# One 512-column matmul for hi and lo of an operand, in a float32 decoder trunk

## The chip, the core and the metric

The kernel runs on one core of one Trainium2 chip. Its time is the device time of one execution in microseconds (us). Engines are named as the profile names them: PE is the tensor engine's matmul, PEld its weight load, DVE the vector engine, ACT the scalar engine, POOL is GpSimd, and SP issues the DMAs.

## The reference

A trunk of two layers over 256 tokens of 2048 features, all in float32. The first mixer is a Conformer convolution, the second an attention with shared K and V (16 query heads, 4 K/V heads of 128 features); after each comes a squared-ReLU MLP with a hidden layer of 8192.

```python
def reference(x, ...):                      # cut to what matters
    h = x
    h = h + conformer_conv(rmsnorm(h, norm_mix[0]), ...)        # y @ w_in, gate, 31 taps, layernorm, silu, @ w_out
    h = h + sq_relu_mlp(rmsnorm(h, norm_mlp[0]), ...)           # relu(y @ w1) ** 2 @ w2
    k_sh, v_sh = shared_kv(h, kv_norm, w_kv, cos, sin)
    h = h + dilated_attn_layer(rmsnorm(h, norm_mix[1]), k_sh, v_sh, attn_w_q[0], attn_w_o[0], cos, sin)
    h = h + sq_relu_mlp(rmsnorm(h, norm_mlp[1]), ...)
    return rmsnorm(h, final_norm)
```

## The kernel before

Activations lie feature-major: tile k of an activation holds features 128k to 128k+127 on the partitions and the 256 tokens along the free dimension. Weights come as chunks of 1 MB: [128, 16 x 128] float32 holds all 2048 inputs of 128 output features. The list `order` fixes their sequence: 32 chunks of w_in, 16 of w_out, 128 of the first MLP, 4 for K, 4 for V, 16 of w_q, 16 of w_o and 128 of the second MLP.

A product is made exact to about float32 by splitting both operands, v = hi + lo, where hi is v rounded to the one-pass format float32r. `split_upto` does that for a chunk: ACT writes hi (L138), DVE or, for the chunks in POOL_LO, GpSimd writes lo (L140). `split_into` and `scaled_split` do the same for an activation tile, which then is [128, 2, 256]: hi in the first 256 columns, lo in the second (L205, L206, L211, L212). `product` adds, for each of the 16 K tiles, three matmuls of 256 columns into one half of a PSUM bank: hi weights times hi, hi weights times lo (L193, L194), lo weights times hi (L195).

A PSUM tile `ps` is one bank, [128, 512] float32; there are eight. Weight buffers are eleven: four chunks are split ahead (LOOK), up to three are raw (RAWS). So hi of the chunk four ahead is written when the product now ending has given its own buffers back.

In `mlp`, the hidden layer is made in four quarters. A quarter is 16 products of the up half (`in_m_in`), each followed by `finish` (DVE L516: relu times the norm's scale; ACT L518: square; split into a tile of `hid`), then 16 products of the down half (`in_m_out`), each added to the residual stream `h` by `add_residual` (DVE L477). The down half's first product needs all 16 `hid` tiles. `project` runs the output product of a mixer: its first four output tiles advance together over 13 K tiles, as the operand is made, and the other tiles follow one by one. In the attention each pair of heads takes two products; a product is copied out by ACT (L673), rotated by four DVE operations (`rotate`, L558 to L561), and later scored (PE L620).

The program is recorded in source order, and a scheduler then sets the order on each engine; where rows below show an engine's order, it is the scheduler's.

Of the kernel before, what the change touches and what calls it, by code (L numbers as in the profile page):

```python
# [18 lines left out]
P = 128  # L19
D = 2048  # L20
T = 256
KT = D // P          # feature tiles of the residual stream
# [7 lines left out]
FQ = 4               # quarters of the MLP's hidden layer  # L30
# [4 lines left out]
# Columns of the packed per-feature vectors: 16 feature tiles each.  # L35
# [5 lines left out]
LOOK = 4             # weight chunks split ahead of the one in use  # L41
RAWS = 3             # weight chunks on their way or waiting to be split
N0 = 4               # output tiles of a product that starts while its operand is still being made
LAST = 13            # K tiles before this one run for all of those

# The first mixer. Its products and its depthwise convolution keep every engine busy, so:
S1_PLAIN = {0, 1, 2, 3, 4, 5, 11, 28}   # chunks of its first product that run as float32
POOL_LO = (set(range(36)) - {28}) | set(range(183, 202, 2))   # chunks (here and in the attention) that GpSimd splits
SLOTS = 8            # partial sums of the convolution that one reduction adds up
# Per reduction: taps that ScalarE multiplies, and how many of them GpSimd adds to others, which makes  # L50
# room for as many more.
PIECES = [(6, 1), (5, 2)]
PE_TAPS = {15: (18, [(6, 1)])}   # feature tiles with taps on the tensor engine: how many, and their PIECES
DIAGS = {11: [15]}   # during which tile those taps' diagonals are made
Y_SPLIT = {0: 2, 1: 9, 2: 16}   # operand tiles that are split by the end of a feature tile
SHIFT = 10           # feature tiles whose mean is the LayerNorm's provisional one
CENTER = {12: [0, 3, 7], 13: [1, 2, 5, 6], 14: [4, 12, 13], 15: [8, 9, 10, 11, 14, 15]}   # when tiles are centered
AHEAD = {13: 31, 14: 34, 15: 34}   # chunks split after a feature tile's gate, where not the next tiles'
# [3 lines left out]
def decoder_kernel(ctx, tc, xT, vec, rope, mask, w_in, w_out, w_k, w_v, w_q, w_o, m_in, m_out, out):  # L62
    """Activations lie feature-major: tile k of a [2048, 256] activation holds features
    128k..128k+127 on the partitions and the 256 tokens along the free dimension. A weight chunk
    [128, 16, 128] holds all of K for 128 output features, so one PSUM tile [128, 256] accumulates
    over its 16 K tiles.

    float32 products: both operands are split exactly, v = hi + lo, hi = v rounded to float32r's 12
    significant bits and lo = v - hi (which has 12 at most), and x.w = xh.wh + xl.wh + xh.wl, each an
    exact one-pass product that is summed in float32. What is left, xl.wl, is below float32's last  # L70
    place of x.w. Attention's own products and a part of the first one, where the vector engine is
    short of time, run as plain float32.
    """
# [30 lines left out]
    def load():  # L104
        """Load as many chunks as there is room for. Those that are not split take a split one's place."""
# [15 lines left out]
    def free(split):  # L121
        live[split] -= 1
        load()

    def split_upto(n):
        """Make the chunks before the n-th ready for use."""
        while len(ready) < min(len(order), n):
            load()
            i = len(ready)
# [42 lines left out]
    def col(name, f):  # L172
        c = VCOL[name] + f
        return vecs[:, c:c + 1]
# [593 lines left out]
```

## Time and profile before

| | |
|---|---|
| time, median of 3 runs (range) | 2118.87 us (2116.08 to 2118.92) |
| span of the profiled execution | 2114.3 us; the runs' times lie 1.8 to 4.6 us above it |
| PE busy | 2058.0 us, 97% of the span |
| DVE / ACT / POOL busy | 59% / 45% / 10% |
| granted PE clock, mean | 0.991 of 2.4 GHz |
| DMA | 368 MB, mean 174 GB/s |

Busy time of PE counts a matmul from its start to its modelled end, so two that follow each other overlap in the records; what a matmul costs is the distance from its start to the next one's start.

### The profile page before, as it was taken

What the parts mean: (1) busy time and instruction counts of PE and PEld (TensorE: products, weight loads), DVE (VectorE), ACT (ScalarE), POOL (GpSimd) and SP (SyncE); (2) the same over time, 40 slices, a digit from 0 to 9 for tenths busy, and PEclk for the clock granted to TensorE, in tenths of its full rate; (3) what the DMA queues carried; (4) which work ended last, traced back from release to release, by engine and by line L of the source; (5) the groups of instructions that cost most, each with busy time, mean ns of one, the idle gap of its engine ahead of it and who ended that gap; (6) DMA issues with size and microseconds to landing.
All of it is one profiled execution on the core that took longest, in us unless ns stands there. A gap on an engine that the chain in (4) does not pass through costs nothing.

```text
span 2114.3 us, 37655 instructions
## 1 busy us (share of the span) xinstructions
PE 2058.0 (97%) x16630; PEld 2032.8 (96%) x16630; DVE 1256.0 (59%) x1499; ACT 955.6 (45%) x1192; POOL 213.0 (10%) x83
## 2 busy tenths in 40 slices
PE   8989799999999999999999999999999999999997
PEld 7888799999999999999999889999999999999997
DVE  7999975554554455445565876555455445545553
ACT  4677664443343344344453554444344334434442
POOL 2687500000000000000003220000000000000000
PEclk9999899999999999999999999999999999999999
DMA  7344235555555555555444334555455545555552
GB/s 285 140 146 153 102 127 186 181 188 182 180 182 188 188 180 180 184 189 186 180 180 179 140 140 149 190 180 180 180 183 189 187 179 181 184 190 184 180 181 79
DMA packets 51619, 368.01 MB, mean 174 GB/s; under 512 B 5856, under 2 KB 5856, under 8 KB 7552
## 3 DMA queue, kind: packets, MB, share of 16 engines
q1 hardware_dynamic: 51312, 365.60, 48.1%
q8 instruction: 130, 2.13, 0.4%
q14 instruction: 33, 0.27, 0.0%
q10 hardware_dynamic: 144, 0.01, 0.0%
HBM read 363.49 MB, written 2.10 MB: 173 GB/s over the span
## 4 chain that ended last, share of the span: by engine, by line
PE 49%; issue 36%; DVE 12%; ACT 2%; POOL 0%; POOLq 0%; DVEq 0%; ACTq 0%
PE ps L193 16%; PE ps L194 15%; PE ps L195 15%; DVE ps L329 3%; DVE prod L335 2%; DVE act L335 2%; DVE sh L559 1%; ACT hi L138 1%; ACT prod L303 1%; DVE prod L329 1%; DVE act L361 0%; PE ps L620 0%; PE ps L593 0%; PE ps L591 0%; PE ps L592 0%
## 5 line engine op out<-in xcount | busy, mean ns | idle before, releaser
L193 PE MATMUL ps<-act,hi 128*128 128x256 f32 x5312 | 1507.5, 284 | 2.7 <-ACT act L205 2.7
L195 PE MATMUL ps<-act,lo 128*128 128x256 f32 x5312 | 1502.2, 283 | 3.0 <-DVE lo L140 3.0
L194 PE MATMUL ps<-act,hi 128*128 128x256 f32 x5312 | 1501.6, 283 | 0.0
L138 ACT CAST hi<-raw 128x2048 fp32r<-128x2048 f32 x336 | 640.0, 1905 | 948.8 <-PE ps L194 791.6
L194 PEld LDWEIGHTS ps<-act,hi 128*128 128x128 f32 x5312 | 1018.0, 192 | 0.6
L195 PEld LDWEIGHTS ps<-act,lo 128*128 128x128 f32 x5312 | 1014.2, 191 | 3.7 <-DVE lo L140 3.4
L193 PEld LDWEIGHTS ps<-act,hi 128*128 128x128 f32 x5312 | 1013.3, 191 | 3.9 <-ACT act L205 3.1
L140 DVE TENSOR_TENSOR lo<-raw,hi 128x2048 fp32r<-128x2048 f32 x298 | 682.9, 2292 | 395.9 <-ACT hi L138 395.8
L477 DVE TENSOR_TENSOR h<-ps,h 128x256 f32<-128x256 f32 x144 | 61.0, 424 | 214.0 <-PE ps L195 213.8
L140 POOL TENSOR_TENSOR lo<-raw,hi 128x2048 fp32r<-128x2048 f32 x38 | 175.0, 4609 | 126.5 <-ACT hi L138 66.3
L226 POOL TENSOR_TENSOR rc<-ms,neg_half 128x2 f32<-128x2 f32 x5 | 3.6, 729 | 1703.4 <-DVE ms L255 1703.4
L516 DVE SCALAR_TENSOR_TENSOR t<-ps,t 128x256 f32<-128x256 f32 x128 | 54.2, 425 | 161.5 <-PE ps L195 161.5
L303 ACT ACTIVATE prod<-u,vecs 128x256 f32<-128x256 f32 x217 | 90.5, 497 | 58.0 <-DVE u L397 53.8
L329 DVE SCALAR_TENSOR_TENSOR ps<-u,vecs,ps 128x256 f32<-128x256 f32 x197 | 79.6, 483 | 0.0
L199 PE MATMUL ps<-act,raw 128*128 128x256 f32 x256 | 59.4, 393 | 6.5 <-DVE act L280 6.5
L199 PEld LDWEIGHTS ps<-act,raw 128*128 128x128 f32 x256 | 50.3, 198 | 13.7 <-DVE act L280 6.5
L206 DVE TENSOR_TENSOR act<-t,act 128x256 fp32r<-128x256 f32 x144 | 60.3, 420 | 0.9 <-ACT act L205 0.9
L205 ACT CAST act<-t 128x256 fp32r<-128x256 f32 x144 | 58.6, 407 | 4.5
L335 DVE TENSOR_REDUCE prod<-prod 128x256 f32<-128x2048 f32 x15 | 58.1, 3873 | 1.6 <-ACT prod L303 0.5
L518 ACT ACTIVATE t<-t 128x256 f32<-128x256 f32 x128 | 52.7, 412 | 4.8 <-DVE t L516 4.8
L335 DVE TENSOR_REDUCE act<-prod 128x256 f32<-128x1536 f32 (+1 forms) x16 | 47.0, 2939 | 0.4
L243 ACT ACTIVATE t<-h 128x256 f32<-128x256 f32 x80 | 31.5, 407 | 28.2 <-DVE h L477 22.2
(103 smaller groups left out, 600.9 us busy)
## 6 DMA issues: line engine op xcount, KB each, us to landing
raw<-in_m_in SPq DMA_DIRECT2D x128, 1024.0 KB, 4.8
raw<-in_m_out SPq DMA_DIRECT2D x128, 1024.0 KB, 4.8
raw<-in_w_in SPq DMA_DIRECT2D x31, 1024.0 KB, 4.9
raw<-in_w_out SPq DMA_DIRECT2D x16, 1024.0 KB, 4.9
raw<-in_w_q SPq DMA_DIRECT2D x16, 1024.0 KB, 4.8
raw<-in_w_o SPq DMA_DIRECT2D x16, 1024.0 KB, 4.8
raw<-in_w_k SPq DMA_DIRECT2D x4, 1024.0 KB, 5.1
raw<-in_w_v SPq DMA_DIRECT2D x4, 1024.0 KB, 4.9
```

The source lines that it names most:

```text
L138: nc.scalar.copy(out=hi, in_=raw)
L140: eng.tensor_tensor(out=lo, in0=raw, in1=hi.bitcast(F32), op=ALU.subtract)
L193: nc.tensor.matmul(ps, lhsT=wh, rhs=a[:, 0, :], start=k == 0, stop=False)
L194: nc.tensor.matmul(ps, lhsT=wh, rhs=a[:, 1, :], start=False, stop=False)
L195: nc.tensor.matmul(ps, lhsT=wl, rhs=a[:, 0, :], start=False, stop=k == KT - 1)
L199: nc.tensor.matmul(ps, lhsT=w[:, k * P:(k + 1) * P], rhs=act_of(k), start=k == 0, stop=k == KT - 1)
L205: nc.scalar.copy(out=a[:, 0, :], in_=src)
L206: nc.vector.tensor_tensor(out=a[:, 1, :], in0=src, in1=a[:, 0, :].bitcast(F32), op=ALU.subtract)
L303: nc.scalar.activation(out=buf[:, i, :], in_=u[:, j:j + T], func=AF.Copy, scale=tap(c, j))
L329: nc.vector.scalar_tensor_tensor(out=a if j < TAPS - 2 else last[:, i % 2, :], in0=x, scalar=tap(c, j), in1=a, op0=ALU.mult, op1=ALU.add)
L335: nc.vector.tensor_reduce(out=dst, in_=buf[:, :n, :].rearrange("p j t -> p t j"), axis=AX.X, op=ALU.add)
L477: nc.vector.tensor_tensor(out=h[:, f, :], in0=ps, in1=h[:, f, :], op=ALU.add)
```

## The change

`product` now passes the whole activation tile, hi and lo side by side, under the hi weights in one matmul of 512 columns, and then hi under the lo weights in one of 256 columns, which adds to the first half of the bank. The second half of the bank holds hi weights times lo. Whoever reads a product adds the halves: `joined` (ACT copies the second half, DVE adds the first) in the MLP's `finish`, for K and for the query heads; the residual additions become two DVE additions each. The old `product` stays as `product3` for the 24 split chunks of w_in; the V product, which never used it, is as it was.

```diff
     def product(ps, w, acts, ks):
+        hi, lo = w
+        for k in ks:
+            wh, wl = hi[:, k * P:(k + 1) * P], lo[:, k * P:(k + 1) * P]
+            a = acts[k]
+            nc.tensor.matmul(ps, lhsT=wh, rhs=a.rearrange("p i t -> p (i t)"), start=k == 0, stop=False)
+            nc.tensor.matmul(ps[:, :T], lhsT=wl, rhs=a[:, 0, :], start=False, stop=k == KT - 1)
+
+    def joined(dst, ps):
+        nc.scalar.copy(out=dst, in_=ps[:, T:])
+        nc.vector.tensor_tensor(out=dst, in0=ps[:, :T], in1=dst, op=ALU.add)
+
+    def product3(ps, w, acts, ks):
         hi, lo = w
...
-                product(ps[:, :T], (hi, lo), y_hl, range(KT))
+                product3(ps[:, :T], (hi, lo), y_hl, range(KT))
...
     def add_bias_residual(f, ps):
-        nc.vector.scalar_tensor_tensor(out=h[:, f, :], in0=ps, scalar=col("bout", f), in1=h[:, f, :],
+        nc.vector.scalar_tensor_tensor(out=h[:, f, :], in0=ps[:, T:], scalar=col("bout", f), in1=h[:, f, :],
                                        op0=ALU.add, op1=ALU.add)
+        nc.vector.tensor_tensor(out=h[:, f, :], in0=ps[:, :T], in1=h[:, f, :], op=ALU.add)
 
     def add_residual(f, ps):
-        nc.vector.tensor_tensor(out=h[:, f, :], in0=ps, in1=h[:, f, :], op=ALU.add)
+        for half in (ps[:, T:], ps[:, :T]):
+            nc.vector.tensor_tensor(out=h[:, f, :], in0=half, in1=h[:, f, :], op=ALU.add)
...
                 r = tmp()
-                nc.vector.scalar_tensor_tensor(out=r, in0=ps, scalar=0.0, in1=rb, op0=ALU.max, op1=ALU.mult)
+                joined(r, ps)
+                nc.vector.scalar_tensor_tensor(out=r, in0=r, scalar=0.0, in1=rb, op0=ALU.max, op1=ALU.mult)
...
-                nc.vector.tensor_tensor(out=ks[:, i, :], in0=ps[:, :T], in1=rb, op=ALU.mult)
+                joined(ks[:, i, :], ps)
+                nc.vector.tensor_tensor(out=ks[:, i, :], in0=ks[:, i, :], in1=rb, op=ALU.mult)
                 rotate(ks[:, i, :])
...
         q = q_of[p][:, i % 2, :]
-        nc.scalar.copy(out=q, in_=ps[:, :T])
+        joined(q, ps)
         rotate(q)
```

In the changed kernel `joined` is L199 (ACT) and L200 (DVE), the wide matmul L194, the narrow one L195; the split's L205 and L206 become L220 and L221, the MLP's L516 and L518 become L534 and L536, and L477 becomes L494.

The scheduler also orders things anew. The first place is PE where a quarter of the MLP passes from its up half to its down half; `ps_8466` (before) and `ps_7074` (of the change) are the down half's first product, `ps_8522` and `ps_7115` its second, `act_8457` and `act_7065` the last `hid` tile, `act_7017` the last but one. Before:

```order
L195 MATMUL ps_8522<-act_7775,lo_8337 128x256
L193 MATMUL ps_8522<-act_7837,hi_8336 128x256
L194 MATMUL ps_8466<-act_8457,hi_8274 128x256
L195 MATMUL ps_8466<-act_8457,lo_8275 128x256
L194 MATMUL ps_8522<-act_7837,hi_8336 128x256
L195 MATMUL ps_8522<-act_7837,lo_8337 128x256
```

Of the change:

```order
L194 MATMUL ps_7115<-act_7017,hi_6972 128x512
L195 MATMUL ps_7115<-act_7017,lo_6973 128x256
L194 MATMUL ps_7074<-act_7065,hi_6924 128x512
L195 MATMUL ps_7074<-act_7065,lo_6925 128x256
L194 MATMUL ps_7115<-act_7065,hi_6972 128x512
L195 MATMUL ps_7115<-act_7065,lo_6973 128x256
```

Before, PE turns to the first product's last K tile after a third of the second product; in the change it does so only after 15 K tiles of the first and 15 of the second, and K tile 14 of the first stands behind 10.5 of the second. All eight quarters look like this.

The second place is ACT at the end of the same up half, where `hi_8460` and `hi_7068` are the hi of the chunk four ahead and `t_8453` and `t_7059` the last product's relu. Before:

```order
L138 CAST hi_8398<-raw_8216 128x2048
L518 ACTIVATE t_8393<-t_8391 128x256
L205 CAST act_8395<-t_8393 128x256
L138 CAST hi_8460<-raw_8278 128x2048
L518 ACTIVATE t_8455<-t_8453 128x256
L205 CAST act_8457<-t_8455 128x256
```

Of the change:

```order
L138 CAST hi_7068<-raw_6928 128x2048
L536 ACTIVATE t_7015<-t_7011 128x256
L199 COPY t_7059<-ps_7026 128x256
L220 CAST act_7017<-t_7015 128x256
L536 ACTIVATE t_7063<-t_7059 128x256
L220 CAST act_7065<-t_7063 128x256
```

Before, the square and the split of a `hid` tile follow right behind the hi of one chunk; in the change the copy of the last product stands behind that hi and the square of the tile before it.

The third place is DVE over the same stretch. Before:

```order
L516 SCALAR_TENSOR_TENSOR t_8453<-ps_8404,t_3800 128x256
L140 TENSOR_TENSOR lo_8461<-raw_8278,hi_8460 128x2048
L206 TENSOR_TENSOR act_8457<-t_8455,act_8457 128x256
L477 TENSOR_TENSOR h_75<-ps_8466,h_75 128x256
L140 TENSOR_TENSOR lo_8517<-raw_8340,hi_8516 128x2048
L477 TENSOR_TENSOR h_75<-ps_8522,h_75 128x256
L140 TENSOR_TENSOR lo_8573<-raw_8402,hi_8572 128x2048
```

Of the change:

```order
L140 TENSOR_TENSOR lo_7069<-raw_6928,hi_7068 128x2048
L200 TENSOR_TENSOR t_7059<-ps_7026,t_7059 128x256
L221 TENSOR_TENSOR act_7017<-t_7015,act_7017 128x256
L534 SCALAR_TENSOR_TENSOR t_7059<-t_7059,t_3528 128x256
L221 TENSOR_TENSOR act_7065<-t_7063,act_7065 128x256
L494 TENSOR_TENSOR h_75<-ps_7074,h_75 128x256
L494 TENSOR_TENSOR h_75<-ps_7115,h_75 128x256
L494 TENSOR_TENSOR h_75<-ps_7074,h_75 128x256
L494 TENSOR_TENSOR h_75<-ps_7115,h_75 128x256
L140 TENSOR_TENSOR lo_7110<-raw_6976,hi_7109 128x2048
L140 TENSOR_TENSOR lo_7151<-raw_7024,hi_7150 128x2048
```

Before, the relu was read from PSUM ahead of the chunk's lo; in the change the reading stands behind that lo, and the next two chunks' lo stand behind the residual additions of the down half's first two products.

## Rows read from the trace of the kernel before

**Rows 1.** The page: busy time by engine, and the chain that ended last.

```profile
PE 2058.0 (97%) x16630; PEld 2032.8 (96%) x16630; DVE 1256.0 (59%) x1499; ACT 955.6 (45%) x1192; POOL 213.0 (10%) x83
...
PE 49%; issue 36%; DVE 12%; ACT 2%; POOL 0%; POOLq 0%; DVEq 0%; ACTq 0%
```

**Rows 2.** Stages: us, busy and count of PE, PEld, DVE, ACT, POOL; clock; DMA.

```profile
235.00:290.00 55.00, 44.61 (x285) 42.24 (x284) 46.01 (x84) 31.89 (x65) 13.05 (x7) 0.81 0.13 45
...
368.00:1100.00 732.00, 732.00 (x6126) 732.00 (x6125) 378.50 (x352) 301.81 (x290) 0.69 (x1) 1.00 0.52 184
...
1330.00:2090.00 760.00, 760.00 (x6360) 760.00 (x6359) 387.46 (x356) 312.14 (x300) 0.69 (x1) 1.00 0.51 179
```

**Rows 3.** Groups of instructions, whole span: count, busy us, mean ns, idle before.

```profile
L193 PE MATMUL ps<-act,hi 128*128 128x256 f32 x5312 | 1507.5, 284 | 2.7 <-ACT act L205 2.7
...
L138 ACT CAST hi<-raw 128x2048 fp32r<-128x2048 f32 x336 | 640.0, 1905 | 948.8 <-PE ps L194 791.6 <-issue 115.1 <-PE ps L195 22.4
...
L477 DVE TENSOR_TENSOR h<-ps,h 128x256 f32<-128x256 f32 x144 | 61.0, 424 | 214.0 <-PE ps L195 213.8
...
L212 DVE SCALAR_TENSOR_TENSOR act<-h,vecs,act 128x256 fp32r<-128x256 f32 x64 | 29.5, 478 | 0.0
...
L673 ACT COPY act<-ps 128x256 f32<-128x256 f32 x16 | 5.9, 368 | 25.7 <-PE ps L195 25.7
```

**Rows 4.** Timeline of PE in the V product: start, duration (us), 512-column matmuls.

```profile
1122.71 0.40 PE L591 MATMUL ps<-hi,act 128*128 128x512 f32 x1
...
1123.41 0.40 PE L591 MATMUL ps<-hi,act 128*128 128x512 f32 x1
...
1143.96 0.39 PE L591 MATMUL ps<-hi,act 128*128 128x512 f32 x1
...
1144.64 0.28 PE L193 MATMUL ps<-act,hi 128*128 128x256 f32 x1
```

**Rows 5.** Timeline of PE in w_in's first, plain float32 chunks.

```profile
29.68 1.67 PE L199 MATMUL ps<-act,raw 128*128 128x256 f32 x7
```

**Rows 6.** Timeline around the end of a product in an MLP's up half.

```profile
1000.97 0.28 PE L195 MATMUL ps<-act,lo 128*128 128x256 f32 x1
1000.97 0.19 PEld L193 LDWEIGHTS ps<-act,hi 128*128 128x128 f32 x1
...
1001.09 0.28 PE L193 MATMUL ps<-act,hi 128*128 128x256 f32 x1
...
1001.17 1.91 ACT L138 CAST hi<-raw 128x2048 fp32r<-128x2048 f32 x1 [3.08 <-PE ps L194]
...
1001.29 0.42 DVE L516 SCALAR_TENSOR_TENSOR t<-ps,t 128x256 f32<-128x256 f32 x1 [1.29 <-PE ps L195]
...
1002.98 0.41 ACT L518 ACTIVATE t<-t 128x256 f32<-128x256 f32 x1
...
1003.10 2.29 DVE L140 TENSOR_TENSOR lo<-raw,hi 128x2048 fp32r<-128x2048 f32 x1 [1.39 <-ACT hi L138]
...
1003.42 0.41 ACT L205 CAST act<-t 128x256 fp32r<-128x256 f32 x1
...
1005.31 0.42 DVE L206 TENSOR_TENSOR act<-t,act 128x256 fp32r<-128x256 f32 x1
```

**Rows 7.** Timeline of one pair of heads in the attention, PE, POOL and DVE.

```profile
1204.77 4.60 POOL L140 TENSOR_TENSOR lo<-raw,hi 128x2048 fp32r<-128x2048 f32 x1 [11.27 <-PE ps L644]
...
1205.47 4.18 DVE L559 TENSOR_TENSOR sh<-sh,ropes 32x256 f32<-32x256 f32 x1
...
1209.03 0.59 PE L620 MATMUL ps<-ks,act 128*128 128x256 f32 x2
...
1210.02 0.41 DVE L561 TENSOR_TENSOR act<-act,sh 32x256 f32<-32x256 f32 x1
...
1210.58 1.11 PE L620 MATMUL ps<-ks,act 128*128 128x256 f32 x6 [0.95 <-DVE act L561]
```

**Rows 8.** DMA issues: MLP chunks, KB each, us from issue to landing.

```profile
raw<-in_m_in SPq DMA_DIRECT2D x128, 1024.0 KB, 4.8
```

More of the change, by code (lines that the diff above doesn't have):

```diff
@@ L492, in project @@
         ws = [take() for _ in range(N0)]
-        pss = [ps_tile()[:, :T] for _ in range(N0)]
+        pss = [ps_tile() for _ in range(N0)]
         for k in steps:
@@ L503, in project @@
         for f in range(N0, KT):
-            finish(f, take(), ps_tile()[:, :T], range(KT))
+            finish(f, take(), ps_tile(), range(KT))
             refill()
@@ L524, in mlp @@
                 ps = ps_tile()
-                product(ps[:, :T], take(), acts, range(KT))
-                waiting.append(ps[:, :T])
+                product(ps, take(), acts, range(KT))
+                waiting.append(ps)
                 if q == 0 and f == 0:
@@ L536, in mlp @@
                 ps = ps_tile()
-                product(ps[:, :T], take(), hid, range(KT))
-                add_residual(f, ps[:, :T])
+                product(ps, take(), hid, range(KT))
+                add_residual(f, ps)
                 if q == FQ - 1:
@@ L569, in decoder_kernel @@
         ps = ps_tile()
-        product(ps[:, :T], take(), kv_acts, range(KT))
+        product(ps, take(), kv_acts, range(KT))
         waiting.append((g, ps))
@@ L670, in decoder_kernel @@
         ps = ps_tile()
-        product(ps[:, :T], take(), acts, range(KT))
+        product(ps, take(), acts, range(KT))
         q = q_of[p][:, i % 2, :]
-        nc.scalar.copy(out=q, in_=ps[:, :T])
+        joined(q, ps)
         rotate(q)
```

## The prediction

> **What bounds the kernel now.** I read the page's busy times first. PE has 97% of the span, DVE 59%, ACT 45%, and the chain that ended last is mostly PE and "issue", with DVE at 12% [rows 1]. An average can hide stages, so the table by stage came next. In the long MLP stretches PE has no idle time at all: 6126 matmuls in 732 us, 6360 in 760 us, one every 119.5 ns at the full clock of 2.4 GHz (granted 1.00); DVE is busy about half of that time, DMA too [rows 2]. So in the MLPs, 256 of the 368 chunks, the time is the number of matmul starts times their distance, and nothing else. The end of w_in and the start of w_out (235 to 290 us) is another matter: PE is busy 44.6 of 55 us at a mean clock of 0.81, with DVE at 46 us; there PE waits for its operand [rows 2].
>
> The distance is therefore the price that matters, not the 284 ns that a record lasts [rows 3]. 256 columns at 2.4 GHz are 106.7 ns, so 12.8 of the 119.5 ns are a surplus that each matmul pays. Whether it belongs to the matmul or to its columns decides this change. The V product answers that: its matmuls are of the new kind, 512 columns of float32r, each under freshly loaded weights. 96 of them run from 1122.71 to 1144.64 us, 228.4 ns each; the fastest stretch gives (1144.64 - 1143.96) / 3 = 227 ns, the slowest (1123.41 - 1122.71) / 3 = 233 ns [rows 4]. 512 columns are 213.3 ns, so the surplus is 15 ns, about that of a 256-column matmul: it belongs to the matmul.
>
> The Trainium skill ("TensorE: Matmul & The Clock Gate", section "Wait — 56ns, not 53.3ns?") puts this surplus at about 2.5 ns for a warm matmul, whatever its width. By that rule, dropping one of three matmuls would save 2.5 ns for each K tile, an estimated 12 us in all. The trace has 119.5 where the rule gives 109, so I go by the trace.
>
> **The change, part by part.** *Matmuls.* The first line of the old product has 5312 matmuls, one for each K tile [rows 3]. The 24 split chunks of w_in (384 K tiles) keep three matmuls. The other 4928 are 4096 in the MLPs, 256 in w_out, 256 in w_o, 64 in K, 256 in the query heads. A K tile cost 3 x 119.5 = 358.5 ns; now it costs a wide and a narrow matmul, 228.4 + 119.5 = 347.9. Saved: 10.6 ns. With the V product's fastest stretch it is 12, with its slowest 6. I take the mean over the whole V product, because it spans all sorts of neighbouring work.
>
> Where does it count? In the MLPs always: 4096 x 10.6 = 43.4 us. In w_out and w_o the first four output tiles advance at the pace of their operand over 13 K tiles; 2 x (256 - 52) = 408 K tiles are left, 4.3 us. K: 0.7 us. The query heads need a look at their waits. In each pair PE stops 0.95 us before the scores, released by DVE's last rotation, which comes after a multiplication that takes 4.18 us instead of the usual 0.4, as long as GpSimd's 4.60 us on a chunk's lo beside it [rows 7]. This chain starts at the end of one product and spans the next, so what the spanned product gains becomes waiting. Half the query tiles count: 128 x 10.6 = 1.4 us. Together 4096 + 408 + 64 + 128 = 4696 K tiles, 49.8 us.
>
> *Reading the halves.* Each of the 128 up-half products adds an ACT copy (0.37 us by the copy of a query head) and a DVE addition (0.42 by the residual addition); the relu now reads SBUF, 0.42 to 0.48. Each down-half product, and those of w_out and w_o, adds a DVE addition of 0.42 [rows 3]. In an MLP stretch of 732 us, about 127 products, DVE goes from 378 to some 432 us and ACT from 302 to some 326 [rows 2], against about 711 us of PE. PE covers this, as long as no result is wanted sooner than it comes. In steady state a read-out has several products' time: eight banks, four chunks split ahead. In the query heads the addition stands ahead of a multiplication that waits for GpSimd anyway. The one naked addition is after the last product: 0.4 us.
>
> *The passage from the up half to the down half* is where results are wanted soon. I count from the next product's first matmul, 1001.09 us in [rows 6]. There the chunk's hi runs from 0.08 to 1.99, its lo from 2.01 to 4.30, and the hidden tile is complete at 4.64, its relu having been read at 0.20, ahead of the lo. In the change the copy stands behind hi and a square, and the addition behind lo (the order of ACT and DVE above). Addition done at 4.7, the split of tile 14 at 5.1, relu 5.6, square 6.0, hi of tile 15 at 6.5, lo at 6.9 to 7.0. In source order PE would want tile 14 at 14 x 0.348 = 4.9 and tile 15 at 5.2: a stall of about 1.8 us in each of eight quarters, 14 us. But the scheduler now puts K tile 14 behind 24.5 pairs (8.5 us) and K tile 15 behind 30 (10.4 us). That covers 7.0 with 3.4 us to spare, so I cost it at nothing. What is late next: the first two down-half products end almost together at about 11 us, and two chunks' lo queue behind their additions. With hi (1.9 us) and lo (2.3 us) in turn they are done at about 15 and 17.3 us; PE wants them after four and five products, at 22.3 and 27.8. Covered too.
>
> *Weights from memory.* A chunk lands 4.8 us after its issue, several are on their way at once [rows 8], and DMA is busy 0.52 of the stretch [rows 2]; a product of 5.57 us instead of 5.74 raises that to 0.54.
>
> *Sum.* -49.8 + 0.4 = -49.4 us. The span goes from 2114.3 to 2064.9; with the 4.6 us by which the median lies above the span, **2069.5 us**.
>
> **The rivals.** *Waits eat a part.* If the scheduler's cover fails, the eight quarters give back 14 us; if each query head's addition is paid in full, 16 x 0.42 = 7 more: 2090. For it: additions behind a chunk's lo are new. Against: the 3.4 us of cover.
>
> *The surplus stays with the columns.* Then a wide matmul costs two narrow ones, 239 ns, less at most the 2 ns that a plain float32 record of two passes has over its 213.3 [rows 5]. The gain is 4696 x 2 = 9 us: 2110. Against it stand the V product's 228.4 ns. The rule of the Trainium skill quoted above would end near here, at 2107.
>
> *The wide matmul sheds its surplus.* In the plain float32 chunks a record holds two passes of 256 columns, and seven lie (1.67 - 0.38) / 6 = 215 ns apart (a record lasts 0.38 us) [rows 5]. If a wide matmul ran like that, a K tile would save 24 ns: 4696 x 24 = 113 us, 2006. Against: the V product is the same float32r form and did not.
>
> *Slower: the weight load shows.* In the V product every load lies under a wide matmul; now the load for a wide one lies under a narrow one, and the widths alternate, which no stretch of this kernel does. From the start of a load to the start of its matmul [rows 6] has 1001.09 - 1000.97 = 0.12 us, just a narrow matmul's distance, though the load's record lasts 0.19. If all 0.19 had to pass before the wide matmul, a pair would cost 228 + 190 = 418 ns, 60 more than now: 4696 x 60 = +282 us, 2400. The change loses from 10.6 ns of exposed load onward. Against: loads under narrow matmuls are what the kernel does now, every 119.5 ns.
>
> **How the numbers follow.** Forecast 0.73; waits 0.11; surplus stays 0.05; wide matmul faster 0.05; load shows 0.04; the remaining 0.02 is a loss of the whole gain by several small waits, no change. A difference under 0.2%, 4 us, can't be told from none here. Only the load's case ends slower: faster 0.94, same 0.02, slower 0.04. The forecast's own range comes from the V product's bounds, 4696 x 12 = 56 and 4696 x 6 = 28 us of gain: 2063 to 2091. Some of the lesser waits in the query heads could vanish as PE's order changes, up to 3 us, and the runs spread by 3. So 2057 to 2093 holds forecast and waits, 0.84.
>
> **What would show it.** Right: PE has 16630 - 4928 = 11702 matmuls; in the MLPs wide ones start 227 to 229 ns before the narrow one that follows, narrow ones 119 to 120; a down-half product starts every 5.57 us; no PE idle at the eight passages; the stretch before 235 us is unchanged. Wrong: a pair over 353 or under 346 ns; idle PE released by DVE's L200 or L221 or by ACT's L220 at a passage; the attention's wait before the scores grown by more than 0.3 us a pair.

## The result, and the profile after

| | before | after |
|---|---|---|
| time, median of 4 runs each (range) | 2117.49 us (2116.08 to 2118.92) | 2082.45 us (2082.01 to 2082.67) |
| ratio, 95% interval | | 0.9835 [0.9821, 0.9849] |
| span of the profiled execution | 2114.3 us | 2080.2 us |

The change gains 35.0 us by the medians and 34.1 by the spans, where 49.4 were forecast (the median of before is under the 2118.87 us of the three runs ahead because a fourth one, 2116.11 us, is in this result). The time lies in the range; about three tenths of the gain is missing, and the question of this section is where it went.

Page of the changed kernel, busy times and the chain that ended last (as in [rows 1]):

```profile
PE 2016.3 (97%) x11702; PEld 1776.2 (85%) x11702; DVE 1354.6 (65%) x1807; ACT 979.7 (47%) x1324; POOL 212.9 (10%) x83
...
PE 50%; issue 35%; DVE 12%; ACT 2%; POOL 0%; DVEq 0%; POOLq 0%; ACTq 0%
```

The matmuls are 11702 as counted, PE keeps 97%, and DVE has 98.6 us more. Stages of the changed kernel (columns as in [rows 2]):

```profile
235.00:290.00 55.00, 47.08 (x246) 42.13 (x245) 46.09 (x85) 31.89 (x64) 13.10 (x7) 0.82 0.13 45
...
380.00:1070.00 690.00, 690.00 (x3955) 604.17 (x3954) 407.19 (x464) 302.63 (x341) 0.00 (x0) 1.00 0.55 188
...
1380.00:2060.00 680.00, 680.00 (x3896) 595.40 (x3896) 391.81 (x438) 294.97 (x330) 0.00 (x0) 1.00 0.53 183
```

In both MLPs PE has no idle time, the four passages of each included. A K tile is now two matmuls: 690 / (3955 / 2) = 348.9 ns and 680 / (3896 / 2) = 349.1, against 358.5 before. So 9.5 ns are saved where 10.6 were forecast. PEld fell from 96% to 85%, with two loads for a K tile instead of three.

Groups of the changed kernel (as in [rows 3]):

```profile
L194 PE MATMUL ps<-act,hi 128*128 128x512 f32 x4928 | 1731.3, 395 | 4.9 <-DVE act L221 4.1
L138 ACT CAST hi<-raw 128x2048 fp32r<-128x2048 f32 x336 | 641.0, 1910 | 853.5 <-PE ps L194 691.4
L494 DVE TENSOR_TENSOR h<-ps,h 128x256 f32<-128x256 f32 x288 | 119.6, 424 | 193.4 <-PE ps L195 189.2
...
L200 DVE TENSOR_TENSOR t<-ps,t 128x256 f32<-128x256 f32 x128 | 53.5, 418 | 1.6 <-ACT t L199 1.6
L199 ACT COPY t<-ps 128x256 f32<-128x256 f32 x128 | 45.6, 356 | 0.0
```

The new readings cost what the nearest rows had said, 0.36 us for a copy and 0.42 for an addition. One thing had not been costed: the first matmul that reads a freshly made operand used to need its hi alone and to wait for ACT, 2.7 us in all [rows 3]; the wide one needs hi and lo and waits for DVE, 4.1 us: 3.2 of them at w_out's first matmul, 0.9 in w_o.

The whole difference by stage, from the first matmul of one stage to that of the next, in us, as read from the matmuls' starts in both traces (the last column is worked out from the terms of the forecast):

```
stage                        before    after   difference   forecast
w_in                         268.57   268.84      +0.27       0
w_out                         94.41    94.62      +0.21      -2.15
first MLP                    735.68   716.29     -19.40     -21.7
K                             24.05    23.49      -0.56      -0.7
V                             21.93    21.94      +0.01       0
query heads, scores, mixing  121.72   124.76      +3.04      -1.4
w_o                           99.54   100.81      +1.27      -2.15
second MLP                   738.60   719.66     -18.94     -21.3
final norm                     9.83     9.82      -0.01       0
```

Of the missing 15.3 us, 4.7 lie in the MLPs, 4.4 in the query heads and 5.8 in w_out and w_o, where the change gains nothing or loses; the rest is 0.4 in K and w_in.

**The query heads.** PE has one wait there that the kernel before did not have. Timeline of PE in the changed kernel at the first pair's `flip` (the transposes L663 and L665):

```profile
1148.76 0.28 PE L195 MATMUL ps<-act,lo 128*128 128x256 f32 x1
1156.41 0.47 PE L663 MATMUL ps<-ident,act 128*128 128x128 f32 x1 [7.37 <-DVE act L653]
...
1157.53 0.63 PE L194 MATMUL ps<-act,hi 128*128 128x512 f32 x1
1157.96 0.41 PE L195 MATMUL ps<-act,lo 128*128 128x256 f32 x1
1158.17 0.63 PE L194 MATMUL ps<-act,hi 128*128 128x512 f32 x1
```

Timeline of ACT and DVE there (L642 masks the scores, L648 is the exponential, L577 is a rotation's multiplication, L653 scales with the exponentials' sums):

```profile
1149.00 1.90 ACT L138 CAST hi<-raw 128x2048 fp32r<-128x2048 f32 x1 [4.66 <-issue]
1150.81 0.37 ACT L199 COPY act<-ps 128x256 f32<-128x256 f32 x1
1151.19 1.28 ACT L648 ACT_TABLE_LOAD   x1
1152.48 0.51 ACT L648 ACTIVATE act<-act,mx 128x256 f32<-128x256 f32 x1
...
1145.67 2.27 DVE L140 TENSOR_TENSOR lo<-raw,hi 128x2048 fp32r<-128x2048 f32 x1
...
1148.21 1.12 DVE L642 SCALAR_TENSOR_TENSOR act<-ps,qs,masks 128x512 f32<-128x512 f32 x2
...
1153.69 2.06 DVE L577 TENSOR_TENSOR sh<-sh,ropes 32x256 f32<-32x256 f32 x1
...
1156.02 0.60 DVE L653 TENSOR_SCALAR act<-act,rl 128x256 f32<-128x256 f32 x2
```

Read it backwards from the transposes, in the order of the queues. The scaling that releases them starts at 1156.02, behind a rotation beside GpSimd, 2.06 us. The exponentials stand on ACT behind a chunk's hi, the next head's copy and the load of their table, 1.28 us. The hi starts at 1149.00, right after the product's last matmul, which gives its buffers back; so the exponentials, whose result PE wants as soon as that product ends, can't begin before it ends. On DVE the masks stand behind a chunk's lo. Before, the masks stood ahead of that lo (the maxima that the exponentials need stood behind it), the exponentials stood ahead of that hi and copy, their table was loaded while ACT had nothing else to do, no rotation stood right ahead of the scaling, and PE lost 0.81 us at this flip. Timeline of PE in the kernel before:

```profile
1170.98 0.33 PE L644 MATMUL ps<-ident,act 128*128 128x128 f32 x1 [0.81 <-DVE act L634]
```

Behind the wait of the changed kernel PE runs at the lower of its two clocks, 1.2 GHz: a wide matmul and the narrow one behind it start 1157.96 - 1157.53 = 0.43 us apart instead of 0.23. Stretches of the changed kernel around the end of the new wait and of two others (the granted clock is the third number from the right):

```profile
1153.00:1160.00 7.00, 3.59 (x13) 3.13 (x14) 3.80 (x9) 1.35 (x7) 2.48 (x1) 0.51 0.44 150
...
293.00:300.00 7.00, 5.24 (x21) 4.38 (x21) 7.00 (x11) 6.68 (x10) 0.00 (x0) 0.76 0.94 378
...
1282.00:1287.00 5.00, 4.67 (x18) 4.00 (x19) 5.00 (x10) 4.90 (x7) 0.00 (x0) 0.66 0.96 331
```

**w_out and w_o.** The other two stand where the fifth chunk of each projection is wanted. Timeline of PE in the changed kernel:

```profile
294.96 0.39 PE L195 MATMUL ps<-act,lo 128*128 128x256 f32 x1 [1.76 <-DVE lo L140]
...
1282.33 0.38 PE L195 MATMUL ps<-act,lo 128*128 128x256 f32 x1 [2.35 <-DVE lo L140]
```

PE waits for that chunk's lo in the kernel before too, by 0.75 us in w_out and by 2.22 in w_o, and there its clock stays full. Timeline of PE and a stretch of the kernel before:

```profile
294.25 0.39 PE L195 MATMUL ps<-act,lo 128*128 128x256 f32 x1 [0.75 <-DVE lo L140]
...
1297.16 0.39 PE L195 MATMUL ps<-act,lo 128*128 128x256 f32 x1 [2.22 <-DVE lo L140]
...
1297.00:1302.00 5.00, 4.84 (x40) 4.84 (x41) 5.00 (x10) 4.64 (x5) 0.00 (x0) 1.00 0.99 403
```

The hi of the chunk needs the buffers of the first of the four tiles that advance together. By PE's order that tile now ends later against the others (in w_out 13 matmuls of them are left behind it, 27 before). In w_o seven residual additions of halves stand on DVE ahead of the lo, where four stood before, but the lo starts only 0.1 us later behind its hi for that; PE also has two new waits ahead of this one, 0.92 us for an operand's lo and 0.83 for the chunk's hi. Each of the two waits for the fifth chunk's lo is followed by a stretch in which part of the time ran at 0.5, which the kernel before does not show.

### The profile page after: what moved, and what is told of

Read it like the earlier page. It is cut to its first block, busy times and chain, and to the rows that moved or that the text cites. A ratio compares the mean times of both kernels' runs of the same rounds, so it can differ in the third digit from the quotient of the medians.

```text
span 2080.2 us, 28137 instructions
## 1 busy us (share of the span) xinstructions
PE 2016.3 (97%) x11702; PEld 1776.2 (85%) x11702; DVE 1354.6 (65%) x1807; ACT 979.7 (47%) x1324; POOL 212.9 (10%) x83
## 4 chain that ended last, share of the span: by engine, by line
PE 50%; issue 35%; DVE 12%; ACT 2%; POOL 0%; DVEq 0%; POOLq 0%; ACTq 0%
PE ps L194 31%; PE ps L195 16%; DVE ps L344 3%; DVE prod L350 2%; DVE act L350 2%; DVE sh L577 1%; ACT hi L138 1%; ACT prod L318 1%; DVE prod L344 1%; DVE act L376 0%; PE ps L639 0%; DVE act L221 0%; PE ps L612 0%; PE ps L611 0%; PE ps L610 0%
## 5 line engine op out<-in xcount | busy, mean ns | idle before, releaser
L194 PE MATMUL ps<-act,hi 128*128 128x512 f32 x4928 | 1731.3, 395 | 4.9 <-DVE act L221 4.1
L195 PE MATMUL ps<-act,lo 128*128 128x256 f32 x4928 | 1381.7, 281 | 4.1 <-DVE lo L140 4.1
L194 PEld LDWEIGHTS ps<-act,hi 128*128 128x128 f32 x4928 | 925.1, 188 | 217.7 <-DVE act L221 4.8
L195 PEld LDWEIGHTS ps<-act,lo 128*128 128x128 f32 x4928 | 933.3, 189 | 6.6 <-DVE lo L140 4.7
L494 DVE TENSOR_TENSOR h<-ps,h 128x256 f32<-128x256 f32 x288 | 119.6, 424 | 193.4 <-PE ps L195 189.2
L208 PE MATMUL ps<-act,hi 128*128 128x256 f32 x384 | 113.1, 294 | 0.0
L209 PE MATMUL ps<-act,hi 128*128 128x256 f32 x384 | 110.9, 289 | 0.0
L208 PEld LDWEIGHTS ps<-act,hi 128*128 128x128 f32 x384 | 76.0, 198 | 0.3
L209 PEld LDWEIGHTS ps<-act,hi 128*128 128x128 f32 x384 | 76.0, 198 | 0.3
L536 ACT ACTIVATE t<-t 128x256 f32<-128x256 f32 x128 | 52.5, 410 | 42.5 <-DVE t L534 42.5
L221 DVE TENSOR_TENSOR act<-t,act 128x256 fp32r<-128x256 f32 x144 | 60.1, 417 | 8.3 <-ACT act L220 8.3
```

The costliest lines, as they stand in the source:

```text
L194: nc.tensor.matmul(ps, lhsT=wh, rhs=a.rearrange("p i t -> p (i t)"), start=k == 0, stop=False)
L195: nc.tensor.matmul(ps[:, :T], lhsT=wl, rhs=a[:, 0, :], start=False, stop=k == KT - 1)
L208: nc.tensor.matmul(ps, lhsT=wh, rhs=a[:, 0, :], start=k == 0, stop=False)
L209: nc.tensor.matmul(ps, lhsT=wh, rhs=a[:, 1, :], start=False, stop=False)
L494: nc.vector.tensor_tensor(out=h[:, f, :], in0=half, in1=h[:, f, :], op=ALU.add)
```

## The experiments

The runs of before that belong to the experiments have medians between 2116.2 and 2118.6 us. Stages are compared by the matmuls' starts, as in the table above. Stages that an experiment leaves as they were before the change repeat within 0.05 us, but for w_in, whose code is the same in all of these kernels and which takes 268.6 to 269.8 us. w_out as the change has it takes 94.1 to 94.7 us in five kernels, so its +0.21 us is neither a loss nor a gain that can be told from none.

**Query heads with three narrow matmuls and one copy.**

```diff
-        product(ps, take(), acts, range(KT))
+        product3(ps[:, :T], take(), acts, range(KT))
...
-        joined(q, ps)
+        nc.scalar.copy(out=q, in_=ps[:, :T])
```

> The changed kernel with the query heads alone put back to three narrow matmuls and one ACT copy. Theory A (the missing gain outside the MLPs is new waits and the low clock behind them): the 7.4 us wait of PE before the first flip goes, no low clock near 1153 us, the stretch from the first query product to w_o falls from 124.8 to about 121.7 us, and the time from 2082.4 to about 2079.4. Theory B (wide pairs simply save less there, no wait matters): 256 K tiles lose their 9.4 ns each, and the time rises to about 2084.8.

Measured: 2079.02 us (2078.09 to 2079.44), ratio 0.9815 [0.98, 0.9829]. The heads take 121.71 us again, as before the change; at the flip PE waits 0.83 us, and the clock stays full in the stretch that had 0.51:

```profile
1152.44 0.33 PE L663 MATMUL ps<-ident,act 128*128 128x128 f32 x1 [0.83 <-DVE act L653]
...
1153.00:1160.00 7.00, 6.48 (x54) 6.08 (x52) 5.55 (x7) 3.51 (x6) 4.61 (x1) 1.00 0.19 75
```

**The wide matmul in the MLPs and K alone.** In addition, w_out and w_o go back:

```diff
-            product(ps, w, acts, ks)
+            product3(ps[:, :T], w, acts, ks)
             add(f, ps)
...
-                product(ps, w, acts, [k])
+                product3(ps[:, :T], w, acts, [k])
```

(and their residual additions read one half).

> Wide matmuls only in the two MLPs and in K; query heads, w_out and w_o as before the change. Theory A: 3.0 us back in the query heads, 1.3 in w_o, 0.2 in w_out, so about 2078. Theory B: besides the query heads 408 K tiles of the projections lose 9.4 ns, so about 2088.6.

Measured: 2077.50 us (2077.13 to 2079.82), 0.981 [0.9796, 0.9825]. Heads, w_out and w_o lie within 0.05 us of before, the MLPs within 0.02 us of the changed kernel. So the change loses in these three stages on balance.

**Both halves read, but three narrow matmuls.** This takes the wide matmul away and leaves all the rest of the change:

```diff
-            nc.tensor.matmul(ps, lhsT=wh, rhs=a.rearrange("p i t -> p (i t)"), start=k == 0, stop=False)
+            nc.tensor.matmul(ps[:, :T], lhsT=wh, rhs=a[:, 0, :], start=k == 0, stop=False, skip_group_check=True)
+            nc.tensor.matmul(ps[:, T:], lhsT=wh, rhs=a[:, 1, :], start=False, stop=False, skip_group_check=True)
...
```

> Three narrow matmuls as before the change, but hi weights times lo goes to the second half of the bank, and every reader adds the halves as in the change: the reading alone. Theory A (reading is covered in the MLPs; their gain fell short by the price of a pair): the MLP stretches take 735.7 and 738.6 us as before the change, within 0.5, and only the query heads and projections lose, 3 to 9 us in all: 2120 to 2127. Theory B (the 5 us that the MLPs fell short by are the reading): the MLP stretches take 738.2 and 741.1, the whole about 5 us more.

Measured: 2124.44 us (2123.37 to 2125.52), 1.003 [1.0018, 1.0041]. The first MLP differs by -0.04 us from before, the second by +0.42, one DVE addition at its end, where nothing covers it. Its matmul price, by the two MLP stretches of this kernel, is 690 / 5773 and 680 / 5691 = 119.5 ns:

```profile
380.00:1070.00 690.00, 690.00 (x5773) 690.00 (x5772) 395.41 (x448) 292.74 (x331) 0.00 (x0) 1.00 0.52 184
1380.00:2060.00 680.00, 680.00 (x5691) 680.00 (x5690) 383.58 (x426) 289.87 (x326) 0.63 (x1) 1.00 0.52 184
```

The heads take 4.26 us more than before and w_o 2.55, with two matmuls that start 6.9 us apart at the first flip. So the losses there come with the reading of the halves and the order that the scheduler makes of it, not with the wide matmul.

**The passage in source order.** The first two products of each down half are kept in the order in which they are written (`product` passes both of its matmuls through the function that it is given):

```diff
-                product(ps, take(), hid, range(KT))
+                product(ps, take(), hid, range(KT), tc.keep_in_program_order if f < 2 else lambda i: i)
```

> The changed kernel with the matmuls of the first two down-half products of each quarter kept in source order, so that the scheduler can't put the last two K tiles behind the second product. If the order covers the late hidden tiles as the prediction reckoned, PE now waits about 1.8 us in each of eight quarters for tiles 14 and 15: 2082.4 + 14 = about 2097. If the tiles are ready in time anyhow, there is no wait and the time stays at 2082.

Measured: 2094.08 us (2093.45 to 2094.95), 0.9887 [0.9872, 0.9901]; the MLPs take 12.7 us more than in the changed kernel, 1.6 us a passage. PE's waits of this kernel in the first MLP (waited for: us in all, times, longest), and its stretch:

```profile
PE ps L194 <- DVE act L221: 4.2, 4, 1.1
...
380.00:1070.00 690.00, 685.75 (x3917) 598.50 (x3917) 404.57 (x459) 299.25 (x338) 0.00 (x0) 1.00 0.55 186
```

The wait is where it was worked out, on the last `hid` tile's lo. The order alone decides it. In the changed kernel that lo comes at the forecast time. Timeline of DVE at the first passage, whose down half begins on PE at 453.98:

```profile
456.01 2.29 DVE L140 TENSOR_TENSOR lo<-raw,hi 128x2048 fp32r<-128x2048 f32 x1 [2.29 <-ACT hi L138]
458.22 0.42 DVE L200 TENSOR_TENSOR t<-ps,t 128x256 f32<-128x256 f32 x1
...
460.23 0.43 DVE L221 TENSOR_TENSOR act<-t,act 128x256 fp32r<-128x256 f32 x1 [0.92 <-ACT act L220]
```

460.66 - 453.98 = 6.7 us, where 6.9 to 7.0 were forecast and PE wants it after 10.4.

**First four output tiles narrow.** The MLP-only version with the wide matmul given to the 12 output tiles of w_out and w_o that run alone:

```diff
-            product(ps, w, acts, ks)
+            if f < N0:
+                product3(ps[:, :T], w, acts, ks)
+            else:
+                product(ps, w, acts, ks)
             add(f, ps)
```

> From the version with the wide matmul in the MLPs and K alone (2077.5 us). Here w_out and w_o get it too, for the 12 output tiles that run alone; the first four, which advance together, keep three narrow matmuls, and so do the query heads. Theory A (the loss in w_out and w_o came only from the first four tiles and how the scheduler finishes them; the other tiles gain as in the MLPs): 2 x 12 x 16 = 384 K tiles x 9.4 ns = 3.6 us less, 2073.9 us; w_out and w_o 1.8 us shorter each than before, PE's wait for the fifth chunk's lo as before (about 1 us), no stretch of granted clock 0.5 near 296 and 1283 us. Rival B (any saved matmul time in w_out and w_o comes back as waiting for the chunks' lo): 2077 to 2079, w_out and w_o as long as before or longer.

Measured: 2075.69 us (2075.28 to 2076.14), 0.9806 [0.9792, 0.9819]; the span is 1.6 us below that of the MLP-only version. w_out gains 0.99 us and w_o 0.34, against 1.8 each. In w_out the wait for the fifth lo is 0.76 us again, with full clock behind it. In w_o it is as long as before the change, 2.23 us against 2.22, but here the granted clock is 0.72 around its end:

```profile
1276.38 0.38 PE L195 MATMUL ps<-act,lo 128*128 128x256 f32 x1 [2.23 <-DVE lo L140]
...
1276.00:1282.00 6.00, 5.62 (x23) 4.82 (x24) 6.00 (x10) 5.62 (x5) 0.00 (x0) 0.72 0.89 335
```

Rival B falls, since both stages gain. Of theory A the waits came as expected, and 1.3 us of the 3.6. In w_o it isn't a longer wait that takes the rest, but the low clock, at least in part; what takes it in w_out is not shown.

**Heads 0 to 3 narrow, the rest wide,** everything else as in the changed kernel:

```diff
+        if i < 4:
+            product3(ps[:, :T], take(), acts, range(KT))
+            nc.scalar.copy(out=q, in_=ps[:, :T])
+        else:
+            product(ps, take(), acts, range(KT))
+            joined(q, ps)
```

> The changed kernel, but with three narrow matmuls and one copy for query heads 0 to 3; heads 4 to 15 keep the wide one. Theory A (the query heads lose by the first pair's flip alone, whose transposes the scheduler put 21 matmuls behind the scores instead of 44; with narrow heads 0 to 3 they stand 44 behind them again): the wait of 7.4 us and the stretch of clock 0.5 at 1153 us are gone, the query heads take 1 to 5 us less than before (3 us more in the changed kernel): 2074 to 2079 us. Rival B (every pair loses by the additions and the shorter products): the query heads take no less time than before, 2079 us or more, with new waits of PE for DVE or ACT at several pairs.

Measured: 2076.27 us (2074.87 to 2077.32), 0.9808 [0.9795, 0.9821]. The heads take 119.21 us, 2.51 less than before. Timeline of PE, the first flip and the scores of the second and third pair:

```profile
1151.55 0.33 PE L663 MATMUL ps<-ident,act 128*128 128x128 f32 x1 [0.81 <-DVE act L653]
...
1159.35 0.89 PE L639 MATMUL ps<-ks,act 128*128 128x256 f32 x4 [0.66 <-DVE act L579]
1174.80 0.92 PE L639 MATMUL ps<-ks,act 128*128 128x256 f32 x4 [0.76 <-DVE act L579]
```

So a wide head is a gain once the pairs run in their steady order, and its wait ahead of the scores is even below the 0.95 of [rows 7]. The heads lose by the order at the first pairs: with heads 0 to 3 narrow they take 5.6 us less than in the changed kernel.

The other gain of this kernel is in w_o. Its code there is the changed kernel's, and PE has the same three waits, 0.92, 0.83 and 2.35 us, but the clock stays full behind them (the last section shows the rows). w_o takes 99.15 us, 1.66 less than in the changed kernel and 0.39 less than before. Up to the third wait the matmuls of the two kernels start at the same distances from w_o's first; the difference arises in the matmuls behind it. So the changed kernel's loss in w_o is the low clock; the waits alone leave a small gain.

**ACT's order at the first pair,** with all heads wide. The first pair's exponentials, the hi of the chunks and the copies of heads 2 and 3 keep the order of the source on ACT:

```diff
-            nc.scalar.copy(out=hi, in_=raw)
+            keep(nc.scalar.copy(out=hi, in_=raw))
...
     for i in range(NH):
         p = i // 2
+        kept[0] = 2 <= i <= 3
```

(`keep` passes its instruction to `tc.keep_in_program_order` while `kept` is set; the copy in `joined` and the exponentials are wrapped likewise.)

> The changed kernel, all query heads with the wide matmul, but ACT keeps the order of the source while heads 2 and 3 are made: the first pair's exponentials stand ahead of the next chunk's hi and of the next head's copy. (With that the scheduler also puts the first pair's masks on DVE ahead of a chunk's lo, and its scaling ahead of it.) PE's order up to the first flip is unchanged, 21 matmuls between scores and transposes. Theory A (the wait of 7.4 us at the first flip comes from the exponentials standing on ACT behind a hi that waits for the end of the product): the wait falls to 2.5 us or less, the clock of 0.5 that followed it goes, the query heads take 5 to 8 us less: 2075 to 2078 us. Rival B (it comes from the transposes standing too close behind the scores on PE): the wait stays over 4 us, 2080 or more. Rival C (the hi that now starts later is late for its own product): the first wait goes, but a new one of several us appears within the next two products, 2080 or more.

Measured: 2083.72 us (2083.11 to 2084.33), 0.9839 [0.9822, 0.9855]. Timeline of PE and of ACT (here L669 is the transpose, L654 the exponential, L144 a chunk's hi, L205 a head's copy, L651 the maxima, L583 a rotation's multiplication, L659 the scaling) and of DVE:

```profile
1149.56 0.33 PE L669 MATMUL ps<-ident,act 128*128 128x128 f32 x1 [0.56 <-DVE act L659]
1172.49 0.45 PE L669 MATMUL ps<-ident,act 128*128 128x128 f32 x1 [8.25 <-DVE act L659]
...
1164.28 0.37 ACT L205 COPY act<-ps 128x256 f32<-128x256 f32 x1 [2.42 <-PE ps L201]
1164.55 1.90 ACT L144 CAST hi<-raw 128x2048 fp32r<-128x2048 f32 x1
1166.35 0.51 ACT L654 ACTIVATE act<-act,mx 128x256 f32<-128x256 f32 x1
...
1165.27 0.67 DVE L651 TENSOR_REDUCE mx<-act 128x2 f32<-128x512 f32 x1
...
1167.43 3.87 DVE L583 TENSOR_TENSOR sh<-sh,ropes 32x256 f32<-32x256 f32 x1
...
1172.01 0.60 DVE L659 TENSOR_SCALAR act<-act,rl 128x256 f32<-128x256 f32 x2
```

The wait at the first flip falls from 7.37 to 0.56 us with PE's order up to there unchanged: A's forecast for this wait came true and B falls, so the wait came from the order on the engines that feed PE. That it was ACT's order alone isn't shown: with the edit the table is loaded ahead of time, too, and on DVE a chunk's lo and the rotation now stand behind the scaling. And a like wait, 8.25 us, now stands at the second flip. Its exponentials were free to go behind a product's copy and a hi, and went there, but that held them up by 0.4 us only, from the end of the first maxima at 1165.94 to 1166.35; most of this wait is DVE's rotation beside GpSimd, 3.87 us, which stands ahead of the scaling. In sum nothing is gained. C foresaw a wait elsewhere, but not for its reason: no product waits for the late hi.

**The price of a K tile.** In the changed kernel's MLPs a wide matmul starts 232.2 ns before the narrow one and that 117.0 ns before the next wide one (means over the first MLP), not 228.4 and 119.5. The order of matmuls was changed first:

```diff
-        for k in ks:
...
+        for two in (ks[i:i + 2] for i in range(0, len(ks), 2)):
+            for k in two:
...
+                nc.tensor.matmul(ps, lhsT=wh, rhs=acts[k].rearrange("p i t -> p (i t)"), start=k == 0, stop=False)
+            for k in two:
...
+                nc.tensor.matmul(ps[:, :T], lhsT=wl, rhs=acts[k][:, 0, :], start=False, stop=k == KT - 1)
```

> The changed kernel with the order of matmuls altered: for every two K tiles the two wide matmuls, then the two narrow ones. In the changed kernel's MLPs a wide one starts 232.2 ns before the narrow one behind it, and that one 117.0 ns before the next wide one: 349.2 ns for a K tile, where the V product (wide after wide, 228.4) and the kernel before (narrow after narrow, 119.5) gave 347.9. Theory A (the difference comes from the change of width between neighbours): with wide after wide half of the time and narrow after narrow half of the time a K tile takes 0.65 ns less at least, 348.5 or below, and down to 346.5 if each neighbourhood keeps its shortest distance; x 4700: 3 to 13 us less, 2069 to 2079 us. Rival B (a K tile costs 349.2 ns in whatever order, so the difference lies in the operands or in the pair's total): MLP stretches as in the changed kernel within 0.5 us; 2082, apart from what other waits do in the query heads.

Measured: 2089.05 us (2088.62 to 2089.87), 0.9865 [0.9851, 0.988]. The first MLP's stretch:

```profile
380.00:1070.00 690.00, 690.00 (x3931) 602.15 (x3930) 405.07 (x458) 300.73 (x340) 0.00 (x0) 1.00 0.55 188
```

690 / (3931 / 2) = 351.1 ns, dearer than in turn. Both theories fall: neighbours of the same width don't help. A wide matmul takes 233.5 ns ahead of a wide one here, too, whose weights are then loaded under a wide matmul as in the V product; so the load is not what makes 228 into 232.

The other trail was the place of the operand. The distances repeat with the activation tiles, in every product alike, and the pattern has the period five in which the tiles' pools alternate. Two kernels move the pools; nothing else changes:

```diff
+    nc.gpsimd.memset(pool("pad", 1).tile([P, 24], F32, name="pad"), 0.0)
     act2 = pool("act2", 8)
```

> The changed kernel with 96 bytes per partition left unused ahead of the second pool of activation tiles, and nothing else. In the changed kernel's MLPs the distance from one wide matmul to the next repeats with a period of five: 347, 347, 354, 348, 352 ns. Every fifth tile comes from the second pool, whose tiles begin 0 bytes behind a multiple of 128, those of the first pool 96 bytes; the 354 is the second pool's tile, the 352 stands two behind it. Theory A (the break between the two offsets costs the time): with one offset every K tile takes 346.7 ns, 2.5 less on the mean, x 4700 = 11.8 us: 2070.7 us. Rival B (offsets don't matter; the price is that of alternating widths): 2082.4, within 1 us, period of five unchanged or its pattern tied to another thing.

and, with a second pad of 8 columns ahead of the weights' pool:

> The changed kernel with the weights' and both activation pools moved so that all their tiles begin at a multiple of 128 bytes. Theory A (only the break between two offsets costs): as with one offset of 96, 346.7 ns for every K tile, 2070.7 us. Theory C (the offset 0 is itself the dear one, 354 ns a tile): 354 - 349.6 = 4.4 ns more on each of 4700 K tiles, 2103 us. Theory D (96 is the dear one and an aligned operand cheaper): under 2068 us. Rival B (offsets don't matter): 2082.4.

Measured: 2084.49 us (2083.41 to 2084.89), 0.9847 [0.9833, 0.986], and 2084.67 us (2083.61 to 2085.02), 0.9848 [0.9834, 0.9861]. The first MLP's stretch in the one and in the other:

```profile
380.00:1070.00 690.00, 690.00 (x3949) 604.14 (x3948) 406.58 (x464) 301.75 (x341) 0.00 (x0) 1.00 0.55 188
```

```profile
380.00:1070.00 690.00, 690.00 (x3950) 603.99 (x3948) 406.22 (x462) 302.37 (x341) 0.00 (x0) 1.00 0.55 188
```

The pattern changes in both (a K tile now takes from 338 to 362 ns, with the longest two behind the shortest), but the mean is 690 / (3949 / 2) = 349.5 ns and 349.4, some 0.5 more and not 2.5 less. Theories A, C and D fall. B's 2082.4 is 2 us short too, since the place moves the pattern and slightly the mean. What makes a wide matmul of this kernel 4 ns dearer than that of the V product stays open. The V product's own distances lie on two levels: 66 of 95 are 226 or 227 ns, the other 29 are 228 to 236, 232.4 on the mean; the MLPs' wide matmuls stand at the dearer level throughout.

**What was seen to gain, together:** the MLPs, K, the 12 lone tiles of both projections, heads 4 to 15 (the edits of "first four output tiles" and "heads 0 to 3" in one kernel).

> Wide matmuls wherever they were seen to gain: MLPs, K, the 12 output tiles of w_out and w_o that run alone, query heads 4 to 15; three narrow ones for the first four output tiles of w_out and w_o and for query heads 0 to 3. Theory A (the stages' gains add): against the changed kernel w_out 1.2 us less, w_o 1.6, query heads 5.5: span 2080.2 - 8.3 = 2071.9, time about 2073, below all kernels so far. Rival B (the heads' end and w_o's start share their waits, so that the gains overlap): 2075 to 2077.

Measured: 2074.13 us (2073.45 to 2074.53), 0.9794 [0.978, 0.9809], the lowest of all, and clearly under the changed kernel's ratio. Its interval overlaps that of the kernel with heads 0 to 3 narrow, though. The span is 2072.4 us against 2080.2; w_out's gain (0.78 us) and the heads' (2.47) stay about as they were alone, w_o is 0.12 us over before. Theory A holds but for w_o. Against the kernel with heads 0 to 3 narrow, w_out gains 0.50 us and w_o loses 0.51, so that narrow first tiles add nothing that shows beside narrow first heads.

## Why the prediction was right, and what it got wrong

**Right: the mechanism and the main term.** The surplus belongs to the matmul, and PE's starts set the time of the MLPs. They give 38.8 of the 43.4 us (with the 0.42 us of the last addition set apart, which the kernel with halves and narrow matmuls shows bare). The surplus that stays with the columns would have given 9 us, the wide matmul that sheds its surplus 113, the exposed load a loss; none came. (The MLPs are 256 of 344 chunks by the list `order`, not of 368; nothing in the sum hangs on that.) The Trainium skill ("TensorE: Matmul & The Clock Gate", "Wait — 56ns, not 53.3ns?") would have given 2.5 ns a K tile for the dropped matmul; the trace has 9.5.

**Mis-sized: the price of a K tile,** 349.0 ns and not 347.9. The row of the V product was the right one to read, and its bounds (6 to 12 ns saved) hold the measured 9.5; the sum was made at its mean, which mixes two levels, and the wide matmul with an activation as moving operand is 4 ns dearer, the narrow one behind it 2.5 cheaper. That is 4.7 us of the 15.3. The signs for single distances missed (227 to 229 and 119 to 120 ns forecast, mostly 230 to 236 and 117 measured), while their sum lies within its bounds. A little luck is in the time: the forecast puts the median 4.6 us above the span, the changed kernel's lies 2.2 above it, so the time is 12.9 us off where the span is 15.3.

**Right: reading is covered in the MLPs** (halves with narrow matmuls: -0.04 us), and **the passage is covered by the scheduler's order** (source order: +12.7 us against 14 forecast).

**Wrong: the query heads, -1.4 forecast and +3.0 measured.** The step that failed is "in the query heads the addition stands ahead of a multiplication that waits for GpSimd anyway", and with it the view that the heads' waits stay what they were. The part of it about the scores was right: their wait fell. What was not looked at is the other end of a pair's chain, the flip, where ACT's order put the first pair's exponentials behind a hi, a copy and a table load, and DVE's order put their scaling behind a multiplication beside GpSimd: 7.37 us of waiting with a low clock behind it. The order of ACT was on hand before the run and was shown for the passage alone. For pairs in steady order the forecast was too low: 12 wide heads gain 2.5 us where half of their K tiles would give 1.0.

**Wrong: w_out and w_o, -4.3 forecast and +1.5 measured.** The step took the other tiles' 408 K tiles as bound by PE. In both projections PE waits for the fifth chunk's lo, a wait that the trace of before already had, 0.75 us in w_out and 2.22 in w_o. Time saved ahead of such a wait comes back as waiting, and the new order lengthened it, to 1.76 and 2.35 us, and put two shorter ones ahead of it in w_o. The forecast had no term for the clock either: in the changed kernel it falls behind both waits, and where it doesn't, with heads 0 to 3 narrow, w_o is 1.66 us shorter and both stages together gain 0.7 us. With the first four tiles narrow and all heads narrow the gain is 1.3 us of 3.6.

The rival "waits eat a part" is thus half of the story: not by additions paid at every head nor at the passages, but at three places in stages that are 15% of the span.

## What to carry to other kernels

Price a new shape of matmul from the distance of starts in the same kernel, and keep its spread as the range: the long steady stretches here came out a tenth short of their forecast gain. In stages where PE already waits, don't multiply instructions by a saving; follow each queue that feeds the wait, and read its order in the changed program for every pair or tile that differs from the steady state, the first above all. Where a scheduler orders the work, use the new form only where it gains: here, leaving it out at the first two pairs of heads gave 7.1 us of span more than using it throughout, and leaving it out at the first tiles too gave 7.8 (the 0.7 us between the two lie in w_in, whose code is the same).

## What the runs showed of the hardware that was not expected

The distance between two matmuls' starts is not one number for a shape. In MLP products with full clock and no idle time, wide ones stand 230 to 236 ns ahead of the narrow one, with the same values at the same activation tile in each product; moving the tiles in memory changed which tile gets which value, and the mean by 0.5 ns.

The price of a wait in PE is not only its length. In the stretch from 1153 to 1160 us, in which the wait of 7.37 us ends, the granted clock was 0.51, from 293 to 300, around the end of one of 1.76 us, 0.76, and in the 5 us about the end of one of 2.35 us 0.66. Yet the wait of 2.22 us in the kernel before left the clock at 1.00, and in the kernel with heads 0 to 3 narrow the same wait of 2.35 us at the same matmul did, which made w_o 1.66 us shorter:

```profile
1276.82 0.39 PE L195 MATMUL ps<-act,lo 128*128 128x256 f32 x1 [2.35 <-DVE lo L140]
...
1276.00:1282.00 6.00, 5.18 (x30) 4.59 (x31) 6.00 (x10) 5.91 (x7) 0.00 (x0) 1.00 0.94 363
```

No run here tells what decides between the two.
